# Remainder products behind the rounded ones in the first column tile of a dense stage, in a one-core decoder step

## The chip, the core and the metric

The kernel runs on one NeuronCore of a Trainium2 chip. The metric is device time in microseconds (us) of one execution. The profile shows the engines of the core: PE (TensorE, matrix products; PEld its weight loads), DVE (VectorE), ACT (ScalarE), POOL (GpSimd) and SP (the queue that issues most transfers), and the DMA engines.

## What is computed

One inference step of a decoder layer for two groups that share weights: 1024 prompt rows of width 1024, and 8 sample rows, each with 8192 cached positions. In the reference, cut to the parts around the change:

```python
xp = xp + merge_heads(fox_prompt(q, k, v, logf), sgu_prompt(u, z, w_s[l], b_s[l]), ...)
xp = xp + cross_attend(rmsnorm(xp, g_cross[l]), mk, mv, w_cq[l], w_co[l])   # q = xn @ w_cq
f, conv_p = conv_ffn(rmsnorm(xp, g_ffn[l]), ..., w_up[l], conv_w[l], conv_b[l], w_down[l])  # h = xn @ w_up
xp = xp + f
```

The same is done for the sample rows, whose attention reads the paged cache (`cache_k`, `cache_v`).

## The kernel before

The prompt rows are handled in two halves of 512. After the attention of both halves, each half goes through `merge`, `out_proj` (weights `w_o`), `cross` (cross-attention) and `ffn` (gated MLP with a convolution). All is written out by hand as Python generators; `yield` hands back a rough cost, and a loop at the end slips steps of the sample rows' work (`decode`: gather of cached keys, the product with the query at L1422 and the sum at L1426 on DVE, and later the product with the values at L1474 on PE) between steps of the prompt's. The recording layer then plans the whole program with a simulated timeline and fixes the order of the instructions on each engine; at run time every engine works through its own list in that order, and waits on semaphores.

Dense products are made nearly as exact as float32 by splitting each operand into a rounded part (float32r, written by ACT) and a remainder (written by DVE), and summing three products: rounded by rounded, and each remainder by the other's rounded part. For weights, `split` does this at L235 (ACT) and L236 (DVE), for scaled operands at L238 (ACT) and L239 (DVE). `gemm3` issues the three products, slice by slice, at L272 (rounded weights, rounded rows), L273 (rounded weights, remainder of the rows) and L274 (remainder of the weights, rounded rows).

`norm_T` prepares the normalised rows for `cross` and `ffn`. For the first 256 rows, then the other 256, it turns the rows with PE transposes (L1105), two of the eight 128-wide slices into one PSUM bank, and splits them from PSUM into `hs` (rounded) and `ls` (remainders). After each 256 rows it calls `first`, which issues the first column tile's 8 x 3 products for these rows, each with 256 columns; the later column tiles take all 512 rows at once. `first` runs in four places: `cross` and `ffn` of either half. In the second part of `ffn`'s rows, `ys[2:]` are scaled just before, by ACT (L1035 and L1036).

PSUM tiles come from the pools `ba` and `bb`; `u` are the SBUF buffers of the split rows, `wh` and `wl` those of the split weights, `kv` the buffers of the cached keys and values. L1006 adds a product to the rows (residual).

Of the kernel before, what the change touches and what calls it, by code (L numbers as in the profile page):

```python
# [45 lines left out]
G_MIX, G_CROSS, G_FFN, G_MEM, G_MERGE, B_S, CW, CB = 0, 8, 16, 24, 32, 40, 48, 48 + 132  # L46
# [32 lines left out]
def build(nc, tc, ctx, a, phases=None):  # L79
# [66 lines left out]
    def BK():  # L146
        turn_[0] += 1
        return BB() if turn_[0] % BR == BR - 1 else BA()

    MM = TR = BK  # L150
# [14 lines left out]
    mmul = nc.tensor.matmul  # L165
# [102 lines left out]
    def gemm3(out, pairs):  # L268

        n = len(pairs)  # L270
        for i, (sh, sl, mh, ml) in enumerate(pairs):
            mmul(out, sh, mh, start=(i == 0), stop=False)  # L272
            mmul(out, sh, ml, start=False, stop=False)  # L273
            mmul(out, sl, mh, start=False, stop=(i == n - 1))  # L274

    paused = [False]

# [841 lines left out]
    def cross(xt, sq):  # L1119
        mkn, mkT, mv, pp, pT = ([None] * MH for _ in range(5))  # L1120

        def fetch(h):
            hc = slice(h * MD, (h + 1) * MD)
            mkn[h] = T2().rearrange("p (a b) -> p a b", b=256)
            nc.sync.dma_start(mkn[h], mk_d[:, hc].rearrange("(a p) b -> p a b", p=P))
            mv[h] = T2().rearrange("p (a b) -> p a b", b=256)
            nc.sync.dma_start(mv[h], mv_d[:, hc].rearrange("(a p) b -> p a b", p=P))

        fetch(0)
        fetch(1)  # L1130

        ws = [wload(wpair(a["w_cq"], kk, 0, 512), 1024) for kk in range(4)]
        q2, ps0 = [], MM()

        def products(out, ws, dt_, hs, ls, c):
            cb = slice(dt_ * P, (dt_ + 1) * P)
            gemm3(
                out,
                [(ws[k // 2][0][:, k % 2, cb], ws[k // 2][1][:, k % 2, cb], hs[k][:, c], ls[k][:, c]) for k in range(8)],
            )  # L1140

        hs, ls = yield from norm_T(xt, G_CROSS, lambda hs, ls, c: products(ps0[:, c], ws, 0, hs, ls, c))
        r = rows_rstd(sq, 0, 4)
        rq = sm([P, 4], "rq", 2)
        nc.vector.tensor_scalar(rq, r, 1.0 / 16, None, op0=ALU.mult)
        oh, ol = [], []

        def keys(h):
            tr = TR()
            for dd in range(2):  # L1150
                for mt in range(2):
                    nc.tensor.transpose(
                        tr[:, dd * 256 + mt * P : dd * 256 + (mt + 1) * P], mkn[h][:, mt, dd * P : (dd + 1) * P], ident
                    )
            mkT[h] = T2().rearrange("p (a b) -> p a b", b=256)
            nc.scalar.activation(mkT[h], tr.rearrange("p (a b) -> p a b", b=256), AF.Copy)

        def weigh(h):
            mx = sm([P, 4], "cmx", 2)
            bs = sm([P, 4], "cbs", 2)  # L1160
            pp[h] = U([P, 4, 256])
            l4 = sm([P, 4], "cl", 2)
            r4 = sm([P, 4], "cr", 2)
            for g in range(2):
                sv = BK().rearrange("p (i m) -> p i m", m=256)
                for i2 in range(2):
                    i = g * 2 + i2
                    for dd in range(2):
                        mmul(sv[:, i2, :], q2[h][:, dd, i * P : (i + 1) * P], mkT[h][:, dd, :], start=(dd == 0), stop=(dd == 1))
                g2 = slice(g * 2, g * 2 + 2)  # L1170
                nc.vector.tensor_reduce(mx[:, g2], sv, axis=AX.X, op=ALU.max, negate=True)
                for i2 in range(2):
                    i = g * 2 + i2
                    nc.scalar.activation(bs[:, i : i + 1], mx[:, i : i + 1], AF.Copy, scale=rq[:, i : i + 1])
                for i2 in range(2):
                    i = g * 2 + i2
                    nc.scalar.activation(
                        pp[h][:, i, :], sv[:, i2, :], AF.Exp, bias=bs[:, i : i + 1], scale=rq[:, i : i + 1], accum_out=l4[:, i : i + 1]
                    )
            nc.vector.reciprocal(r4, l4)  # L1180
            for i in range(4):
                nc.scalar.activation(pp[h][:, i, :], pp[h][:, i, :], AF.Copy, scale=r4[:, i : i + 1])

        def turned(h):
            pT[h] = U([P, 2, 512])
            for mt in range(2):
                tr = TR()
                for i in range(4):
                    nc.tensor.transpose(tr[:, i * P : (i + 1) * P], pp[h][:, i, mt * P : (mt + 1) * P], ident)
                nc.scalar.activation(pT[h][:, mt, :], tr, AF.Copy)  # L1190

        def gather(h):
            oh2, ol2 = U([P, 2, 512], F32R), U([P, 2, 512], F32R)
            for dd in range(2):
                ps = BK()
                for mt in range(2):
                    mmul(ps, mv[h][:, mt, dd * P : (dd + 1) * P], pT[h][:, mt, :], start=(mt == 0), stop=(mt == 1))
                split(ps, oh2[:, dd, :], ol2[:, dd, :])
                oh.append(oh2[:, dd, :])
                ol.append(ol2[:, dd, :])  # L1200

        for n in range(2):
            if n:
                ws = [wload(wpair(a["w_cq"], kk, n * 512, 512), 1024) for kk in range(4)]
            for dt_ in range(4):
                if dt_ % 2 == 0:
                    q2.append(U([P, 2, 512]))
                if n or dt_:  # L1210
                    ps = MM()
                    products(ps, ws, dt_, hs, ls, slice(0, 512))
                else:
                    ps = ps0
                nc.scalar.activation(q2[-1][:, dt_ % 2, :], ps[:, :512], AF.Copy)
                yield 5.2
                if n and dt_ == 0:
                    keys(0)
                    keys(1)
                    fetch(2)  # L1220
                if n and 1 <= dt_ < 3:
                    weigh(dt_ - 1)
        keys(2)
        fetch(3)
        turned(0)
        yield 1
        weigh(2)
        yield 3
        gather(0)
        yield 4  # L1230
        keys(3)
        turned(1)
        yield 1
        weigh(3)
        yield 3
        gather(1)
        yield 4
        for h in (2, 3):
            turned(h)
            yield 1  # L1240
            gather(h)
            yield 4
        ys = []
        sq = yield from out_proj(a["w_co"], oh, ol, xt, ys=ys)
        return ys
# [2 lines left out]
    hlast = [const.tile([P, 2 * NF, 2], F32, tag=f"hlast{h}", name=f"hlast{h}") for h in range(2)]  # L1248

    def ffn(hf, xt, ys, late=None):  # L1250
        w0, pv0 = wload(a["w_up"][0], 1024), BK()

        def up(out, w, hs, ls, c):
            hv, lv = (w[q].rearrange("p (k c) -> p k c", c=P) for q in range(2))
            gemm3(out, [(hv[:, k, :], lv[:, k, :], hs[k][:, c], ls[k][:, c]) for k in range(8)])

        hs, ls = yield from norm_T(ys, G_FFN, lambda hs, ls, c: up(pv0[:, c], w0, hs, ls, c))
        if hf:

            fix = sm([P, 2 * NF, 2], "fix", 1)  # L1260
# [8 lines left out]
        for gi, gn in enumerate(GROUPS):  # L1269
            gh, gl = [], []  # L1270
            for f in range(f0, f0 + gn):
                hc2 = []
                for part in range(2):
                    ft = f + part * NF
                    cw = [gp[:, CW + i * 44 + ft : CW + i * 44 + ft + 1] for i in range(3)]
                    cb = gp[:, CB + ft : CB + ft + 1]
                    if ft:
                        w_, pv = wload(a["w_up"][ft], 1024), BK()
                        up(pv, w_, hs, ls, slice(0, 512))
                    else:  # L1280
                        pv = pv0
                    hc = T2()
                    nc.scalar.activation(hc, pv, AF.Identity, bias=cb, scale=cw[2])
                    nc.scalar.activation(hlast[hf][:, ft, :], pv[:, 510:512], AF.Copy)
                    nc.vector.scalar_tensor_tensor(hc[:, 1:], pv[:, :511], cw[1], hc[:, 1:], op0=ALU.mult, op1=ALU.add)
                    nc.vector.scalar_tensor_tensor(hc[:, 2:], pv[:, :510], cw[0], hc[:, 2:], op0=ALU.mult, op1=ALU.add)
                    if hf:
                        nc.vector.tensor_tensor(hc[:, 0:2], hc[:, 0:2], fix[:, ft, :], op=ALU.add)
                    hc2.append(hc)
                    yield 5.2  # L1290
# [11 lines left out]
            for n in range(2):  # L1302
                ws = []
# [8 lines left out]
                for i in range(4):  # L1312
                    tb = slice(i * P, (i + 1) * P)
                    ps = MM()
# [584 lines left out]
    for t in prompt():  # L1899
# [10 lines left out]
        while bgs and not held[0] and most and acc[0] >= PACE[phase[1] or phase[0]]:  # L1910
            most -= 1
            acc[0] -= PACE[phase[1] or phase[0]]
            w = next(bgs[0], None)
# [97 lines left out]
```

## Time and profile before

| | |
|---|---|
| Time, median of 3 runs | 1814.82 us (1810.97 to 1816.68) |
| Profiled execution | 1810.32 us, span of the core 1808.3 us |
| Granted PE clock, mean over the span | 0.989 |
| PE busy | 1741.4 us (96%), 9637 matmuls |
| DVE busy | 1396.9 us (77%) |
| ACT busy | 734.3 us (41%) |
| POOL busy | 501.8 us (28%) |
| Memory | 287 GB/s over the span |

The span is the time from the first to the last instruction of the core. Busy times overlap. In a group of instructions the fields are: line, engine, operation, output<-inputs, form, count; busy us and mean ns of one; idle time of the engine before them, and what ended it. In a timeline row: start in us, length in us, engine, line, operation, and in square brackets the idle time before it and its releaser. `PE bb L273` is the instruction of line 273 that writes a `bb` tile.

### The profile page before, as it was taken

The numbers are of one execution on the slowest core, as the hardware profiler recorded it, in microseconds if no ns is written. First come the engines' busy times: TensorE is split into PE (matmuls) and PEld (weight loads), VectorE is DVE, ScalarE is ACT, GpSimd is POOL, SyncE is SP. The second block draws the span as 40 slices with busy tenths as digits, with TensorE's granted clock in tenths as the row PEclk, the third lists the DMA queues.
The fourth block names the chain that finished last, engine by engine and source line by source line (L and its number), as shares of the span: only waits on it lengthen the run. The fifth ranks groups of instructions, "written<-read, shape, count | busy, mean of one in ns | idle before, by whom it ended". The sixth has DMA issues, their size and how long they took to land.

```text
span 1808.3 us, 25094 instructions
## 1 busy us (share of the span) xinstructions
PE 1741.4 (96%) x9637; PEld 1292.1 (71%) x9637; DVE 1396.9 (77%) x1729; ACT 734.3 (41%) x1378; POOL 501.8 (28%) x461
## 2 busy tenths in 40 slices
PE   8999999878999999999999999989999999999997
PEld 5887776656676767777777776766676678767875
DVE  4689658987788887999989899888875549855344
ACT  6332265465633544433323244235453333232332
POOL 1232333432133433223332233433322111001110
PEclk9999999998999999999999999999999999999999
DMA  7886888786597986778878788979878677568982
GB/s 290 304 304 230 293 316 331 261 278 196 213 404 268 346 315 252 264 280 338 321 278 317 267 313 329 383 285 349 325 283 314 246 289 253 183 260 295 358 314 81
DMA packets 157075, 521.06 MB, mean 288 GB/s; under 512 B 20875, under 2 KB 40843, under 8 KB 124187
## 3 DMA queue, kind: packets, MB, share of 16 engines
q0 software_dynamic: 57168, 341.14, 49.6%
q1 hardware_dynamic: 92874, 165.73, 26.2%
q10 hardware_dynamic: 6912, 12.59, 1.9%
q8 instruction: 76, 1.25, 0.3%
q14 instruction: 45, 0.36, 0.1%
HBM read 495.47 MB, written 23.93 MB: 287 GB/s over the span
## 4 chain that ended last, share of the span: by engine, by line
PE 53%; issue 8%; DMA 6%; DVE 5%; POOL 2%; ACT 2%; POOLq 0%; DVEq 0%; SPq 0%; ACTq 0%
PE ba L274 7%; PE ba L272 7%; PE ba L273 7%; PE bb L273 4%; PE bb L274 4%; PE bb L272 4%; PE dv L1474 4%; DMA kv<-cache_k,io 3%; DMA kv<-cache_v,io 2%; PE dv L321 1%; PE dv L1750 1%; PE ba L1055 1%; PE ba L1054 1%; PE ba L1056 1%; DVE s L1426 1%
## 5 line engine op out<-in xcount | busy, mean ns | idle before, releaser
L235 ACT ACTIVATE wh<-wr 128x1024 fp32r<-128x1024 f32 (+2 forms) x220 | 228.6, 1044 | 490.4 <-PE ba L273 157.7
L236 DVE TENSOR_TENSOR wl<-wr,wh 128x1024 fp32r<-128x1024 f32 (+2 forms) x220 | 262.3, 1198 | 174.0 <-PE ba L274 59.3
L1406 POOL DMA_INDIRECT kv<-cache_k,io x128 | 195.0, 1523 | 562.5 <-DVE s L1426 321.1
L1422 DVE TENSOR_TENSOR kv<-kv,d 128x1024 f32<-128x1024 f32 (+1 forms) x156 | 258.0, 1680 | 29.9 <-DMA kv<-cache_k,io 29.9
L1426 DVE TENSOR_REDUCE s<-kv 128x16 f32<-128x1024 f32 (+1 forms) x156 | 258.1, 1672 | 0.1
L1468 POOL DMA_INDIRECT kv<-cache_v,io x128 | 167.4, 1308 | 276.5 <-PE dv L1474 191.0
L273 PE MATMUL ba<-u,wh 128*128 128x512 f32 (+1 forms) x560 | 219.6, 392 | 1.8 <-DVE u L239 1.5
L272 PE MATMUL ba<-u,wh 128*128 128x512 f32 (+1 forms) x560 | 219.2, 393 | 1.7 <-ACT u L238 1.7
L274 PE MATMUL ba<-u,wl 128*128 128x512 f32 (+1 forms) x560 | 218.7, 392 | 0.0
L272 PE MATMUL ba<-wh,u 128*128 128x512 f32 (+1 forms) x495 | 186.9, 379 | 1.7 <-ACT u L235 1.7
L273 PE MATMUL ba<-wl,u 128*128 128x512 f32 (+1 forms) x495 | 185.5, 375 | 1.2 <-DVE wl L236 1.2
L274 PE MATMUL ba<-wh,u 128*128 128x512 f32 (+1 forms) x495 | 183.8, 376 | 0.0
L1474 PE MATMUL dv<-kv,s 128*32 128x512 f32 x1024 | 125.0, 598 | 2.9 <-DMA kv<-cache_v,io 2.9
L273 PEld LDWEIGHTS ba<-u,wh 128*128 128x128 f32 x560 | 106.0, 189 | 30.3 <-issue 5.2
L273 PE MATMUL bb<-u,wh 128*128 128x512 f32 (+1 forms) x304 | 118.6, 390 | 8.7 <-DVE u L239 8.7
L274 PEld LDWEIGHTS ba<-u,wl 128*128 128x128 f32 x560 | 105.9, 189 | 29.1 <-issue 6.1
L272 PEld LDWEIGHTS ba<-u,wh 128*128 128x128 f32 x560 | 105.9, 189 | 28.7 <-issue 4.0
L272 PE MATMUL bb<-u,wh 128*128 128x512 f32 (+1 forms) x304 | 118.5, 390 | 0.1
L274 PE MATMUL bb<-u,wl 128*128 128x512 f32 (+1 forms) x304 | 117.6, 387 | 0.0
L272 PEld LDWEIGHTS ba<-wh,u 128*128 128x128 f32 x495 | 93.0, 188 | 26.8 <-issue 6.9
L274 PEld LDWEIGHTS ba<-wh,u 128*128 128x128 f32 x495 | 92.8, 188 | 21.5 <-issue 3.8
L273 PEld LDWEIGHTS ba<-wl,u 128*128 128x128 f32 x495 | 93.1, 188 | 20.1 <-DVE wl L236 1.9
(432 smaller groups left out, 3251.0 us busy)
## 6 DMA issues: line engine op xcount, KB each, us to landing
wr<-w_up SPq DMA_DIRECT2D x88, 512.0 KB
kv<-w_up POOLq DMA_DIRECT2D x22, 1024.0 KB
wr<-w_down SPq DMA_DIRECT2D x40, 512.0 KB
kv<-w_down POOLq DMA_DIRECT2D x11, 1024.0 KB
wr<-w_in SPq DMA_DIRECT2D x16, 512.0 KB
wr<-w_o SPq DMA_DIRECT2D x16, 512.0 KB
wr<-w_cq SPq DMA_DIRECT2D x16, 512.0 KB
wr<-w_co SPq DMA_DIRECT2D x16, 512.0 KB
```

The lines of the kernel that those rows point to most:

```text
L235: nc.scalar.activation(h, src, AF.Copy)
L236: nc.vector.tensor_tensor(l, src, h.bitcast(F32), op=ALU.subtract)
L272: mmul(out, sh, mh, start=(i == 0), stop=False)
L273: mmul(out, sh, ml, start=False, stop=False)
L274: mmul(out, sl, mh, start=False, stop=(i == n - 1))
L321: mmul(ps[32 * j : 32 * j + 32, :w], xT[:, k, :] if nk == 8 else xT[:, k * 8 : k * 8 + 32], raw[:, q, j * w : (j + 1) * w], start=(k == 0) ...
L1054: mmul(pss[i], mh[k][:, tb], wh, start=(k == korder[0]), stop=False)
L1406: nc.gpsimd.indirect_dma_start(kv, None, a["cache_k"], off(kidx[:, b, ch : ch + 1]))
L1422: nc.vector.tensor_tensor(kvv[:, i : i + m, :], kvv[:, i : i + m, :], qb.unsqueeze(1).broadcast_to((P, m, 512)), op=ALU.mult)
L1426: nc.vector.tensor_reduce(s[:, ch * 4 + i : ch * 4 + i + m, :].rearrange("p k h -> p (k h)"), kvv[:, i : i + m, :].rearrange("p k (h d) -> ...
L1468: nc.gpsimd.indirect_dma_start(kv, None, a["cache_v"], off(kidx[:, b, ch : ch + 1]))
L1474: mmul(dv[32 * j : 32 * j + 32, :], s[:, ch * 4 : ch * 4 + 4, :].rearrange("p k h -> p (k h)"), kvv[:, j, :], start=(ch == 1), stop=(ch == ...
```

## The change

A second form of the three products, `gemm3_late`, takes a list of outputs. It issues, for every output, the products with rounded rows (with the rounded weights and with the weights' remainders) for all slices, and after those, for every output again, the products with the rows' remainders. The first column tile of `cross` and of `ffn` uses it, in both halves; every other tile keeps `gemm3`. The lists `begun` hold one tile each, so that the number of tiles that are begun in `norm_T` stays one. The sum of the same 24 products is accumulated in another order.

```diff
+    def gemm3_late(outs):
+
+        for out, pairs in outs:
+            for i, (sh, sl, mh, ml) in enumerate(pairs):
+                mmul(out, sh, mh, start=(i == 0), stop=False)
+                mmul(out, sl, mh, start=False, stop=False)
+        for out, pairs in outs:
+            for i, (sh, sl, mh, ml) in enumerate(pairs):
+                mmul(out, sh, ml, start=False, stop=(i == len(pairs) - 1))
...
-        q2, ps0 = [], MM()
-
-        def products(out, ws, dt_, hs, ls, c):
+        q2, begun = [], [MM() for _ in range(1)]
+
+        def pairs(ws, dt_, hs, ls, c):
             cb = slice(dt_ * P, (dt_ + 1) * P)
-            gemm3(out, [... for k in range(8)])
-
-        hs, ls = yield from norm_T(xt, G_CROSS, lambda hs, ls, c: products(ps0[:, c], ws, 0, hs, ls, c))
+            return [... for k in range(8)]
+
+        def first(hs, ls, c):
+            gemm3_late([(ps[:, c], pairs(ws, d, hs, ls, c)) for d, ps in enumerate(begun)])
+
+        hs, ls = yield from norm_T(xt, G_CROSS, first)
...
-        w0, pv0 = wload(a["w_up"][0], 1024), BK()
-
-        def up(out, w, hs, ls, c):
+        begun = {ft: (wload(a["w_up"][ft], 1024), BK()) for ft in (0,)}
+
+        def pairs(w, hs, ls, c):
             hv, lv = (w[q].rearrange("p (k c) -> p k c", c=P) for q in range(2))
-            gemm3(out, [(hv[:, k, :], lv[:, k, :], hs[k][:, c], ls[k][:, c]) for k in range(8)])
-
-        hs, ls = yield from norm_T(ys, G_FFN, lambda hs, ls, c: up(pv0[:, c], w0, hs, ls, c))
+            return [(hv[:, k, :], lv[:, k, :], hs[k][:, c], ls[k][:, c]) for k in range(8)]
+
+        def first(hs, ls, c):
+            gemm3_late([(pv[:, c], pairs(w, hs, ls, c)) for w, pv in begun.values()])
+
+        hs, ls = yield from norm_T(ys, G_FFN, first)
```

In the changed kernel the three lines of `gemm3_late` are 280 (rounded by rounded), 281 (remainder of the weights) and 284 (remainder of the rows).

More of the change, by code (lines that the diff above doesn't have):

```diff
@@ L1132, in cross @@
         ws = [wload(wpair(a["w_cq"], kk, 0, 512), 1024) for kk in range(4)]
-        q2, ps0 = [], MM()
-        def products(out, ws, dt_, hs, ls, c):
+        q2, begun = [], [MM() for _ in range(1)]
+        def pairs(ws, dt_, hs, ls, c):
             cb = slice(dt_ * P, (dt_ + 1) * P)
[L1137 to L1140, printed above, removed]
-        hs, ls = yield from norm_T(xt, G_CROSS, lambda hs, ls, c: products(ps0[:, c], ws, 0, hs, ls, c))
+            return [(ws[k // 2][0][:, k % 2, cb], ws[k // 2][1][:, k % 2, cb], hs[k][:, c], ls[k][:, c]) for k in range(8)]
+        def first(hs, ls, c):
+            gemm3_late([(ps[:, c], pairs(ws, d, hs, ls, c)) for d, ps in enumerate(begun)])
+        hs, ls = yield from norm_T(xt, G_CROSS, first)
         r = rows_rstd(sq, 0, 4)
@@ L1209, in cross @@
                     q2.append(U([P, 2, 512]))
-                if n or dt_:
+                if n or dt_ >= len(begun):
                     ps = MM()
-                    products(ps, ws, dt_, hs, ls, slice(0, 512))
+                    gemm3(ps, pairs(ws, dt_, hs, ls, slice(0, 512)))
                 else:
-                    ps = ps0
+                    ps = begun[dt_]
                 nc.scalar.activation(q2[-1][:, dt_ % 2, :], ps[:, :512], AF.Copy)
@@ L1276, in ffn @@
                     cb = gp[:, CB + ft : CB + ft + 1]
-                    if ft:
+                    if ft in begun:
+                        pv = begun.pop(ft)[1]
+                    else:
                         w_, pv = wload(a["w_up"][ft], 1024), BK()
-                        up(pv, w_, hs, ls, slice(0, 512))
-                    else:
-                        pv = pv0
+                        gemm3(pv, pairs(w_, hs, ls, slice(0, 512)))
                     hc = T2()
```

## The prediction

> **What bounds the kernel now.** I read the page first: busy time, then the chain that ended last.
>
> ```profile
> span 1808.3 us, 25094 instructions
> ...
> PE 1741.4 (96%) x9637; PEld 1292.1 (71%) x9637; DVE 1396.9 (77%) x1729; ACT 734.3 (41%) x1378; POOL 501.8 (28%) x461
> ...
> PE 53%; issue 8%; DMA 6%; DVE 5%; POOL 2%; ACT 2%; POOLq 0%; DVEq 0%; SPq 0%; ACTq 0%
> ```
>
> PE is occupied 96% of the span and carries the largest part of the chain; the last three matmul lines of the dense stages (L272 to L274) are the work that everything else serves. So a microsecond in which PE stands still is, at first sight, a microsecond of the kernel, and only PE's waits can be won. As many weight loads as matmuls were run (9637 each): every product loads its own weights, whatever stood before it, so regrouping products neither saves nor adds a load.
>
> The change touches four places, the first column tile after each of the four row normalisations. Next I read the groups of PE instructions in four stretches of 20 us that begin with the transposes L1105: cross-attention of the first half (546 to 566 us), its feed-forward (702 to 722), cross-attention of the second half (1177.5 to 1197.5) and its feed-forward (1340 to 1360). Of the first three answers stand the rows on which I build, in this order (one, two and one); in the fourth no wait for a remainder stands. The last field is PE's idle time before the group and what ended it.
>
> ```profile
> L273 PE MATMUL bb<-u,wh 128*128 128x256 f32 (+1 forms) x18 | 6.2, 345 | 2.7 <-DVE u L239 2.7
> L273 PE MATMUL ba<-u,wh 128*128 128x256 f32 (+1 forms) x18 | 6.6, 366 | 1.6 <-DVE u L239 1.5
> L1105 PE MATMUL ba<-cp,u 128*128 128x128 f32 x20 | 3.5, 288 | 1.1 <-ACT u L1035 1.1
> L273 PE MATMUL bb<-u,wh 128*128 128x256 f32 x10 | 4.2, 417 | 6.0 <-DVE u L239 6.0
> ```
>
> L273 is the product with the rows' remainder, and L239 on DVE makes that remainder. The waits that the change aims at are therefore 2.7, 1.5 and 6.0 us, 10.2 together. The 1.1 for the scaled rows (L1035) is not its subject. 10.2 us is the ceiling of the direct gain, 0.6% of the kernel. 0.3%, 5.4 us, is about what a measurement of this kernel can tell from no change.
>
> **The change, part by part.** It removes and adds no instruction: 16 products with rounded rows and 8 with remainders in each half of each tile, as before. It moves the eight remainder products behind the sixteen others, so that PE no longer stops at slice 1 while later rounded slices lie ready. What that is worth depends on what comes last in each place.
>
> *Second-half cross-attention* (the 6.0). The timeline, PE, then ACT, then DVE:
>
> ```profile
> 1183.22 0.39 PE L272 MATMUL bb<-u,wh 128*128 128x256 f32 x1
> 1189.11 0.58 PE L273 MATMUL bb<-u,wh 128*128 128x256 f32 x1 [5.50 <-DVE u L239]
> 1189.49 0.42 PE L274 MATMUL bb<-u,wl 128*128 128x256 f32 x1
> 1189.71 0.41 PE L272 MATMUL bb<-u,wh 128*128 128x256 f32 x1
> ...
> 1190.56 1.05 PE L1105 MATMUL ba<-cp,u 128*128 128x128 f32 x4
> 1191.27 0.56 PE L273 MATMUL bb<-u,wh 128*128 128x256 f32 x1
> ...
> 1194.56 0.28 PE L272 MATMUL bb<-u,wh 128*128 128x256 f32 x1
> 1194.68 0.28 PE L273 MATMUL bb<-u,wh 128*128 128x256 f32 x1
> ...
> 1194.91 0.60 PE L1105 MATMUL bb<-cp,u 128*128 128x128 f32 x4
> ...
> 1184.91 0.86 ACT L238 ACTIVATE u<-ba,gp 128x256 fp32r<-128x256 f32 x2
> 1186.32 2.35 DVE L1422 TENSOR_TENSOR kv<-kv,d 128x1024 f32<-128x1024 f32 x2
> 1189.83 0.86 DVE L239 SCALAR_TENSOR_TENSOR u<-ba,gp,u 128x256 fp32r<-128x256 f32 x2
> 1190.62 2.33 DVE L1426 TENSOR_REDUCE s<-kv 128x16 f32<-128x1024 f32 x2
> ...
> 1197.08 0.48 DVE L239 SCALAR_TENSOR_TENSOR u<-bb,gp,u 128x256 fp32r<-128x256 f32 x1 [0.54 <-ACT u L238]
> ```
>
> PE had run slice 0 and the first product of slice 1 when it stopped; 13 products with rounded rows were left, and ACT had rounded all eight slices by 1184.91 + 0.86 = 1185.8. A product takes 0.12 us (1194.56 to 1194.68), so these 13 take 1.6 us and fit into the 5.5 us of idle time. At 1189.1, when DVE delivers slice 1's remainder behind a decode product of 2.35 us, seven remainder products and three groups of four transposes are left. At the slow spacing of this place (0.22 from 1189.49 to 1189.71, 0.71 for a group of transposes from 1190.56 to 1191.27) that is 1.5 + 2.1 = 3.6 us; at the fast product spacing, 0.8 + 2.1 = 2.9. DVE's further remainders (the pair at 1189.83 ends at 1190.7) don't hold it up. The half tile then ends at 1192.0 to 1192.7 in place of 1194.9: 2.2 to 2.9 us. But the other half's remainders stand behind the decode sums on DVE (to 1192.9): six more at 0.39 (a pair takes 0.86, one 0.47) end at 1195.3, where now the last ends at 1197.6. So DVE passes on 2.3 at most. I take 2.0; bounds 1.0 (the transposes, now queued on PE behind the sixteen products, come no earlier) and 2.9.
>
> *First-half cross-attention* (the 2.7).
>
> ```profile
> 558.67 0.39 PE L273 MATMUL bb<-u,wh 128*128 128x256 f32 x1 [2.04 <-DVE u L239]
> 562.50 0.58 PE L273 MATMUL bb<-u,wh 128*128 128x256 f32 x1 [0.37 <-DVE u L239]
> ...
> 564.50 0.39 PE L272 MATMUL bb<-u,wh 128*128 128x512 f32 x1
> 561.97 0.47 DVE L239 SCALAR_TENSOR_TENSOR u<-bb,gp,u 128x256 fp32r<-128x256 f32 x1
> ```
>
> Here DVE sets the end: its last remainder is done at 562.44, and PE starts on it at 562.50. Behind it 14 products run until 564.50, nine of them with rounded rows. Those nine move ahead into the idle time: 9 x 0.12 = 1.1 us. The 2.04 itself isn't won, since the last remainder comes no sooner. Bounds 0 (their rounding is late too) and 2.7.
>
> *The two feed-forwards.* In the first, without the 1.5 us wait PE reaches the next transposes earlier and waits there for L1035, which ACT ends when it does now: 0, bounds -0.3 and 0.5. In the second nothing waits for a remainder: 0, bounds 0 and 0.5.
>
> Sum: 2.0 + 1.1 + 0 + 0 = 3.1 us.
>
> *The clock.* PE's granted clock falls to half after a stretch of 3.41 us in which PE did too little. A row of the stretches gives its bounds, its length, the busy time of PE, PEld, DVE, ACT and POOL, PE's clock, and the DMA's share and rate:
>
> ```profile
> 556.17:559.58 3.41, 1.37 (x8) 0.97 (x7) 3.41 (x7) 1.42 (x3) 1.00 (x1) 1.00 1.01 404
> 559.58:563.00 3.42, 3.05 (x10) 2.24 (x9) 3.42 (x6) 0.00 (x0) 0.00 (x0) 0.50 1.04 402
> 702.94:706.36 3.42, 1.93 (x14) 1.39 (x12) 3.42 (x7) 3.42 (x9) 1.62 (x2) 1.00 1.03 412
> 706.36:709.77 3.41, 1.52 (x9) 1.03 (x8) 1.59 (x4) 3.41 (x10) 0.54 (x1) 1.00 0.99 417
> 1184.20:1187.60 3.40, 0.00 (x0) 0.00 (x0) 3.40 (x6) 1.54 (x4) 0.92 (x1) 1.00 1.02 424
> 1187.60:1191.00 3.40, 1.89 (x9) 1.89 (x10) 3.40 (x8) 0.00 (x0) 1.94 (x1) 0.51 0.30 70
> 1191.00:1194.40 3.40, 3.40 (x17) 3.40 (x17) 2.86 (x5) 1.36 (x3) 0.95 (x1) 0.50 0.64 263
> ```
>
> After 1.93 us of work (702.94) the next stretch had the full clock, after 1.37 (556.17) and after none (1184.20) half: the threshold lies between 1.37 and 1.93. With most of the 13 products (1.6 us in all) the stretch of 1184.20 comes to that edge; with some of the nine (1.1 us) that of 556.17 may pass it. A stretch at half clock spaces products 0.22 instead of 0.12, and so loses about 3.41 x (1 - 0.12/0.22) = 1.5 us, unless a wait covers it, as DVE's last remainder at 562.44 does. I count a quarter of one such stretch, 0.4, bounds 0 and 2 x 1.5 = 3.0. [...]
>
> In all -3.5 us: 1810.32 for the profiled execution becomes 1806.8. That execution lies 4.5 us below the median of the runs (1814.82); from the median, 1811.3.
>
> **The rivals.**
>
> *The clock recovers as well (faster).* The stretches of 1187.60 and 1191.00 run at half clock now. If the early products before them suffice for the full clock, 2 x 1.5 = 3.0 us come on top of 3.5: -6.5, 1808.3, and up to -11 if the upper bounds of both attention terms hold too (0.9 and 1.6 more, and 2 of further waits and a third stretch). For it: 1.6 us more work in a stretch that had none. Against it: the threshold may be above that, and DVE is busy all of 1184 to 1191, so that PE may merely wait at full clock.
>
> *Given back (no change).* DVE, not PE, sets the pace where the change works (3.4 of 3.4 us busy in most of the stretches above). If the other half's remainders, or the next decode step's keys from memory, come when they come now, PE stops a little later: 0 to -1, about 1814.5. The same time follows if the scheduler had not kept the written order; in the built order it did, sixteen products first, with transposes between.
>
> *Reordered decode work (slower).* The scheduler planned the whole program anew. In the built order 322 of DVE's some 1730 instructions change place, though none by more than eleven. In the second half's output projection a decode product pair now goes ahead of a weight remainder (L236) and of a residual add (L1006).
>
> ```profile
> 1174.96 1.23 DVE L236 TENSOR_TENSOR wl<-wr,wh 128x1024 fp32r<-128x1024 f32 x1 [1.56 <-PE ba L1073]
> ```
>
> Each such swap delays what PE waits for by 2.3 us (L1422 above), if DVE has no slack; here it had 1.56 us. Two swaps without slack eat the gain, and from four on (4 x 2.35 - 3.5 = +5.9) the kernel is slower: 1820.7. For it: DVE is 77% busy. Against it: slack as in this row, and equal numbers of moves the other way.
>
> **How the numbers follow.** Forecast 40%, given back 10%, clock 32%, reordered 18%. Forecast and given back lie within 0.3%: 0.50; faster 0.32; slower 0.18. The likeliest case gives 1811.3. The range takes the clock rival down to -11 (1804) and the reordered one up to 1820, which leaves out about 1 in 10 on either side; the forecast alone, its bounds added up without the clock's (0.7 to 6.6 us), spans 1808.2 to 1814.1.
>
> **What would show it.** In the profile after: no wait of 5.5 us before slice 1's remainder product in the second-half cross-attention, but one of some 3 us further on, before line 284, and the tile done 2 to 3 us earlier; in the first half the wait for DVE moves behind the rounded products; in the first feed-forward the wait for L1035's rows grows by what the remainder wait loses. PE's busy time stays at 1741 us, less what the half clock gives back. Wrong would be: the same idle total in the four stretches, PE idle at new places between them, or more stretches at half clock.

## The result, and the profile after

| | before | after |
|---|---|---|
| median | 1815.41 us (1809.38 to 1821.46, 22 runs) | 1807.42 us (1802.23 to 1815.63, 22 runs) |
| ratio | | 0.9966, 95% interval 0.9955 to 0.9976 |
| profiled execution | 1810.32 us, clock 0.989 | 1812.65 us, clock 0.987 |

The changed kernel is faster by about 6 us (0.34% of 1815.4). A second measurement (e7 below) gave 0.9971. The ratio and its interval are formed from all runs of both kernels; they are not the quotient of the two medians, which lie 8.0 us apart. The two profiled executions rank the kernels the wrong way round: that of before lies 5 us under its median, that of after 5 us over. In the 253 runs of the experiments a run's time follows, within a kernel, its mean granted clock by about 1.1 us for each 0.001, and the 22 runs of the changed kernel above cover 0.984 to 0.994. So lengths from the traces are compared below stretch by stretch, and the gain is taken from the runs.

The page of after:

```profile
span 1810.9 us, 25097 instructions
...
PE 1741.1 (96%) x9637; PEld 1295.4 (72%) x9637; DVE 1398.3 (77%) x1729; ACT 735.3 (41%) x1378; POOL 503.7 (28%) x461
...
PE 50%; issue 8%; DMA 8%; DVE 7%; POOL 2%; ACT 1%; POOLq 0%; DVEq 0%; ACTq 0%
```

The matmuls and the instructions of DVE, ACT and POOL are as many as before (the three more in the total are none of these), and PE is busy as long as before. What moved is the order. The timeline of PE in the second cross half, with DVE's decode product of that moment as the last row:

```profile
1184.24 0.38 PE L280 MATMUL bb<-u,wh 128*128 128x256 f32 x1 [0.97 <-ACT u L238]
...
1186.01 0.39 PE L280 MATMUL bb<-u,wh 128*128 128x256 f32 x1 [0.56 <-ACT u L238]
...
1186.81 0.28 PE L284 MATMUL bb<-u,wh 128*128 128x256 f32 x1
1190.08 0.79 PE L284 MATMUL bb<-u,wh 128*128 128x256 f32 x2 [2.99 <-DVE u L239]
...
1193.94 0.56 PE L284 MATMUL bb<-u,wh 128*128 128x256 f32 x1
...
1187.28 2.35 DVE L1435 TENSOR_TENSOR kv<-kv,d 128x1024 f32<-128x1024 f32 x2
```

The wait of 5.50 us is now 2.99, and stands before line 284; 0.97 and 0.56 us of waits for ACT's rounding are new. All sixteen rounded products and slice 0's remainder are done by 1187.1. The last product of the half tile starts 15.25 us after the place's first transpose (1178.69), where it was 17.07 before (1194.79 - 1177.72), and twelve transposes for the next rows now stand ahead of it in place of eight.

The first cross half and the first feed-forward:

```profile
559.39 0.50 PE L273 MATMUL ba<-u,wh 128*128 128x512 f32 x1 [2.44 <-DVE u L239]
710.30 0.33 PE L1115 MATMUL ba<-cp,u 128*128 128x128 f32 x1 [3.09 <-ACT u L1045]
711.27 0.58 PE L280 MATMUL ba<-u,wh 128*128 128x256 f32 x1 [0.64 <-ACT u L238]
```

In the first, the wait is 2.44 us instead of 2.04 and 0.37, and now stands at a 512-column product that the planner put among these. In the second, the wait of 1.47 us for a remainder is gone, and the wait for the scaled rows has grown from 1.12 to 3.09.

The first transposes of the four places cut the span into stretches that can be compared. Before, then after:

```profile
546.12 1.03 PE L1105 MATMUL ba<-cp,u 128*128 128x128 f32 x8
702.22 0.60 PE L1105 MATMUL bb<-cp,u 128*128 128x128 f32 x4
1177.72 0.49 PE L1105 MATMUL ba<-cp,u 128*128 128x128 f32 x3
1340.90 0.60 PE L1105 MATMUL ba<-cp,u 128*128 128x128 f32 x4
```

```profile
546.82 1.03 PE L1115 MATMUL ba<-cp,u 128*128 128x128 f32 x8
704.94 0.60 PE L1115 MATMUL bb<-cp,u 128*128 128x128 f32 x4
1178.69 0.49 PE L1115 MATMUL ba<-cp,u 128*128 128x128 f32 x3
1339.84 0.60 PE L1115 MATMUL ba<-cp,u 128*128 128x128 f32 x4
```

From the first to the second place (cross of the first half) it is 156.1 before and 158.1 after, 2 us more. From the third to the fourth (cross of the second half) it is 163.2 and 161.2, 2 us less. Up to the first place every engine runs the same list, and behind it the planner has ordered the other work anew. So there are two candidates for the gain: the order of the products, and the order of all the rest.

### The profile page after: what moved, and what is told of

Its sections match the earlier page's. It is cut to its first block, busy times and chain, and to the rows that moved or that the text cites. A ratio compares the mean times of both kernels' runs of the same rounds, so it can differ in the third digit from the quotient of the medians.

```text
span 1810.9 us, 25097 instructions
## 1 busy us (share of the span) xinstructions
PE 1741.1 (96%) x9637; PEld 1295.4 (72%) x9637; DVE 1398.3 (77%) x1729; ACT 735.3 (41%) x1378; POOL 503.7 (28%) x461
## 4 chain that ended last, share of the span: by engine, by line
PE 50%; issue 8%; DMA 8%; DVE 7%; POOL 2%; ACT 1%; POOLq 0%; DVEq 0%; ACTq 0%
PE ba L272 6%; PE ba L274 6%; PE ba L273 6%; DMA kv<-cache_v,io 6%; PE dv L1487 3%; PE bb L272 3%; PE bb L273 3%; PE bb L274 3%; DVE s L1439 1%; DVE kv L1435 1%; DVE wl L236 1%; PE dv L331 1%; DMA kv<-cache_k,io 1%; PE dv L1763 1%; POOL kv L1419 1%
## 5 line engine op out<-in xcount | busy, mean ns | idle before, releaser
L1435 DVE TENSOR_TENSOR kv<-kv,d 128x1024 f32<-128x1024 f32 (+1 forms) x156 | 258.1, 1682 | 32.6 <-DMA kv<-cache_k,io 27.3
L273 PE MATMUL ba<-u,wh 128*128 128x512 f32 x528 | 208.5, 395 | 2.4 <-DVE u L239 2.4
L272 PE MATMUL ba<-u,wh 128*128 128x512 f32 x528 | 209.5, 397 | 0.0
L274 PE MATMUL ba<-u,wl 128*128 128x512 f32 x528 | 209.1, 396 | 0.0
L274 PEld LDWEIGHTS ba<-u,wl 128*128 128x128 f32 x528 | 99.2, 188 | 29.1 <-issue 5.7
L273 PEld LDWEIGHTS ba<-u,wh 128*128 128x128 f32 x528 | 99.3, 188 | 27.0 <-DVE u L239 2.6
L272 PEld LDWEIGHTS ba<-u,wh 128*128 128x128 f32 x528 | 99.5, 189 | 25.7 <-issue 4.0
L272 PE MATMUL bb<-u,wh 128*128 128x512 f32 x272 | 108.5, 399 | 0.0
L273 PE MATMUL bb<-u,wh 128*128 128x512 f32 x272 | 108.0, 397 | 0.0
L274 PE MATMUL bb<-u,wl 128*128 128x512 f32 x272 | 107.9, 397 | 0.0
```

Of the source, the lines that this page charges most:

```text
L1435: nc.vector.tensor_tensor(kvv[:, i : i + m, :], kvv[:, i : i + m, :], qb.unsqueeze(1).broadcast_to((P, m, 512)), op=ALU.mult)
```

## The experiments

Times are medians beside runs of the kernel before on the same chip; ratios are to those runs.

**e1 and e2: the new order in one stage only.** In the stage named the list is handed to `gemm3_late`, in the other to `gemm3`:

```diff
-            gemm3_late([(pv[:, c], pairs(w, hs, ls, c)) for w, pv in begun.values()])
+            for w, pv in begun.values():
+                gemm3(pv[:, c], pairs(w, hs, ls, c))
```

> Only the cross stage's first tile takes the new order; the ffn's first tile has the order of before again. Theory (the rounded products fill the waits for the remainders in the two cross places, the ffn places give about nothing): ratio to before 0.9966 to 0.998, that is the whole gain of the full change; in the trace the second cross half shows the wait before L284 of about 3 us and the tile's last product 1 to 2.5 us after the last remainder. Rival, the new plan of the work around (not the order of the products) gives the gain: a ratio that lies anywhere between 0.995 and 1.003, with the waits at the first tiles as in the full change. Rival, the ffn places carry half of the gain: 0.9983.

> Only the ffn's first tile takes the new order; the cross stage's first tile has the order of before again. Theory: no gain, ratio 0.9995 to 1.0005, the 5.5-us wait in the second cross half is there again. Rival, the ffn places carry half: 0.9983. Rival, the new plan: anywhere between 0.995 and 1.003.

e1: 1813.82, ratio 1.0009 (0.9998 to 1.0021). e2: 1817.09, ratio 1.0021 (1.0007 to 1.0035). In e1 the wait of the second cross half has shrunk as in the full change:

```profile
1187.82 0.80 PE L284 MATMUL bb<-u,wh 128*128 128x256 f32 x2 [2.62 <-DVE u L239]
```

And yet nothing is won; e2, where nothing was to be won, loses 3.8 us. The theory missed both. Both lie in what the rival of a new plan allowed (0.995 to 1.003), which is too wide to be a test.

**e3: the remainder last within each slice.** In `gemm3_late` the second loop is dropped, and the remainder product follows the two others of its slice:

```diff
                 mmul(out, sl, mh, start=False, stop=False)
-        for out, pairs in outs:
-            for i, (sh, sl, mh, ml) in enumerate(pairs):
                 mmul(out, sh, ml, start=False, stop=(i == len(pairs) - 1))
```

> Both first tiles, but the product with the remainder is only put last within each slice (three products a slice, slice after slice), so that at most two more rounded products stand before the first wait for a remainder. Theory: the waits for the remainders stay, 5.2 to 5.5 us in the second cross half and 2 us in the first; ratio 0.9995 to 1.0003. Rival, any new order of these products makes the program around it be planned anew and that gives the gain: 0.996 to 0.998 as in the full change.

1807.91, ratio 0.9979 (0.9965 to 0.9992), not what the theory expected, with the big wait in place:

```profile
1184.41 0.58 PE L282 MATMUL bb<-u,wh 128*128 128x256 f32 x1 [5.33 <-DVE u L239]
```

So a kernel can win 3.8 us without filling the wait, and another can fill it and win none. Each of these small edits makes the planner order the program anew, and the results scatter by 4 us either way.

**e4: two tiles begun.** `range(2)` in place of `range(1)` for `begun` in `cross`, and `(0, NF)` in place of `(0,)` in `ffn`.

> The new order, with two tiles begun instead of one in both stages: the rounded products of two tiles (32 per half tile instead of 16) stand before the first product with a remainder. Theory: in the second cross half the rounded products of the second tile lie in the 3.0-us wait that the full change leaves, 16 of 0.12 us = 1.9 us, and in the first half the 2.4-us wait shrinks by as much; together 2 to 4 us below the full change, ratio to before 0.9945 to 0.9960. Rival, what bounds the place is not the remainders but the clock that is halved there: then PE does the same work at half speed and the ratio is that of the full change, 0.9966. Rival, the second tile's weights or bank come late or keep a bank from the work around: above 0.998.

1814.03, ratio 1.0012 (0.9993 to 1.0031): the theory missed it. PE's idle time in the 20 us from each place is the least of all (0.8, 3.7, 3.2 and 0.6 us, against 2.4, 3.7, 4.5 and 2.5 in e7, the changed kernel again), and the kernel is no faster than before. Its trace has a new wait that begins 72 us behind the third place. PE's row, then ACT's:

```profile
1258.01 6.59 PE L1179 MATMUL ba<-t,u 128*128 128x256 f32 x16 [7.79 <-ACT t L1166]
...
1255.93 1.06 ACT L235 ACTIVATE wh<-wr 128x1024 fp32r<-128x1024 f32 x1 [3.11 <-DMA wr<-w_co]
...
1257.37 0.59 ACT L1166 ACTIVATE t<-ba 128x512 f32<-128x512 f32 x1
```

PE waits for a copy by ACT, and in ACT's list a rounding of weights stands ahead of it that itself waits 3.11 us for the weights. So here too the order of the rest weighs against what the places win. e4 also runs 96 more matmuls (9733), as a tile that is begun takes 256 columns at a time. What each of the two costs was not measured.

**The order of the rest held still.** To part the two candidates, the program is planned once in each order of the products, the two plans are taken as lists of instructions for every engine, and the kernel proper is chained to a list put together from them:

```diff
+    for e, q in plan.items():
+        for x, y in zip(q, q[1:]):
+            tc.add_manual_dep(traced[y], x, info, reason="plan")   # y behind x on engine e
```

In the stretch of a first tile PE's list takes the tile's products from one plan; everything else on PE, and all of ACT, DVE, POOL and SP, comes from the other. In the first two kernels the row transposes among the products counted as part of the rest.

> The new order of the products in all four places, but every other instruction of every engine keeps the order that it has in the kernel before (the order is written out and each engine's list is chained to it). Theory of the prediction (the rounded products lie in the waits for the remainders): the whole gain of the order is here, 2.5 to 3.5 us, ratio 0.9981 to 0.9986; the second cross half shows a wait of about 3 us before L284 in place of 5.5 us before L273. Rival, the gain of the full change comes from the decode and prompt work that the planner orders anew behind the first place: ratio 0.9997 to 1.0005 here.

> The reverse: the three products of each slice stand together as in the kernel before, but every other instruction of every engine has the order of the changed kernel. Theory of the prediction: no gain, ratio 0.9995 to 1.0005, and the wait of 5 us or more before the remainder's product is there again. Rival, the new order of the other work gives the gain: 0.9966 to 0.9982, the same as the full change.

> The changed kernel itself, measured beside the two. It was 0.9966 (0.9955 to 0.9976) of the kernel before, with a mean clock of 0.9888; at the same granted clock the two differ by 3.2 us, 0.9982. Theory and rival both expect 0.9965 to 0.9985; it says whether the two kernels beside it, with one half of the change each, add up to it.

e5: 1812.47, ratio 0.9992 (0.9978 to 1.0006). e6: 1819.74, ratio 1.0031 (1.0014 to 1.0049). e7: 1810.18, ratio 0.9971 (0.9957 to 0.9985). Neither half alone is the change: e5 lies between its theory and its rival, and e6 misses both, being slower than before. In e5 the wait stayed:

```profile
1184.67 1.09 PE L1124 MATMUL ba<-cp,u 128*128 128x128 f32 x4 [5.21 <-DVE rq L1165]
```

It is now a transpose that waits. Before, four transposes for the next 256 rows stood between slice 3's products; they wait for DVE, and in e5 they were left there, with nine of the sixteen rounded products behind them. The planner of the full change had put them behind the rounded products. So e5 left undone a part of what the change does.

**e8 to e10: the transposes as well.** In e8 and e9 the transposes among the products go with them.

> As e5 (new order of the products, the rest in the order of before), but the row transposes that stand among a first tile's products also take the place that they have in the changed kernel: in the second cross half they stand behind the rounded products. e5 had kept them in front of the last rounded products, and there the 5.2-us wait stayed. Theory: the gain is in the tile's own stretch, products and transposes together: the 5.2-us wait shrinks to about 3 us and the ratio falls from 0.9992 to 0.9975 to 0.9983. Rival, the order of the other work behind the first places gives the rest: ratio 0.9988 to 0.9996, as e5.

> As e6 (products slice by slice, the rest in the order of the changed kernel), with the row transposes too in the place that they have in the kernel before. Theory: without the new order there is no gain, 0.9995 to 1.0005. Rival, the order of the other work has a gain of its own: 0.9975 to 0.9985. Third, that order fits only the new order of the products, as e6 with 1.0031 looks: 1.0015 to 1.0035 again.

> The remainder's product last within each slice, as in e3, but every other instruction keeps the order of the kernel before. e3, planned anew, had 0.9979 with the waits for the remainders all but unchanged. If that gain came from the order of the other work, this kernel has none: 0.9995 to 1.0005. If it came from the products themselves: 0.9975 to 0.9985.

e8: 1811.61, ratio 0.9984 (0.9969 to 1.0000). e9: 1814.87, ratio 1.0015 (0.9999 to 1.0030). e10: 1814.53, ratio 1.0003 (0.9987 to 1.0019). The waits of the second cross half in e8 and e10:

```profile
1184.83 0.61 PE L282 MATMUL bb<-u,wh 128*128 128x256 f32 x2 [2.97 <-DVE u L239]
```

```profile
1187.62 0.80 PE L282 MATMUL bb<-u,wh 128*128 128x256 f32 x2 [5.47 <-DVE u L239]
```

e10 answers e3: with the rest held still, the order within a slice shows no gain, so e3's 3.8 us needed the rest planned anew. e8 gives the worth of the new order with the rest of before, about 2.9 us (0 to 5.6); the interval covers its theory and its rival, and by time e8 cannot be told from e5, though the wait fell from 5.21 to 2.97 us. The rest of the changed kernel does not pay by itself (e9).

**e11 and e12: the new rest in the second half only.** On every engine the two plans hold the same instructions up to a point some 30 us ahead of the third place. The list is the plan of before up to there, that of the change behind it.

> The new order of the products, with the rest in the order of the kernel before up to some 30 us ahead of the second cross half, and from there in the order of the changed kernel (both lists hold the same instructions up to that point on each engine). In the traces the stretch from the first row transpose of the first cross half to that of the first ffn half takes 156.1 and 156.1 us with the order of before (the kernel before, e8) and 158.1 and 158.7 us with the new one (the changed kernel, e7), the stretch from the second cross half to the second ffn half 163.2 and 164.9 against 161.2 and 160.9 us. Theory: the order of the rest that comes with the change loses 2 us in the first stretch and wins 2 to 4 us in the second; with the better of each this kernel lies 1.5 to 3 us below the changed kernel, ratio 0.9950 to 0.9963. Rival: such differences of single executions are the clock's, and the order of the rest has no part: 0.9984 as e8.

> The same order of the rest as e11, but the three products of each slice stand together as in the kernel before, with the row transposes in their old place. Against e11 it is the price of the order of the products with all else the same; against the kernel before it is the price of the order of the rest in the second half. Theory: the order of the products carries 2 to 3.5 us, so 0.9975 to 0.9990 here. Rival, the order of the rest is worth something only with the new order of the products (e9 was at 1.0015): 0.9998 to 1.0010.

e11: 1806.69, ratio 0.9959 (0.9946 to 0.9972). e12: 1813.40, ratio 0.9996 (0.9983 to 1.0010). e11 is as its theory had it and excludes its rival; e12 lies nearer to its rival. All in one table, ratios to the kernel before:

| rest of the program | old order of the products | new order | worth of the new order |
|---|---|---|---|
| as before | 1 | 0.9984 (e8) | -0.16%, 2.9 us |
| new in the second half | 0.9996 (e12) | 0.9959 (e11) | -0.37%, 6.7 us |
| new | 1.0015 (e9) | 0.9971 (e7), 0.9966 | -0.44 to -0.49%, 8 to 9 us |

The new order pays in each row. By the means of the listed runs, with 1.96 standard errors, it is worth 2.5 ± 2.2, 6.9 ± 1.9 and 8.5 ± 2.9 us. The new rest in the second half adds 4.5 us to it (e8 to e11; 5.6 ± 2.6 by the means), but next to nothing without it (e12). That the order is worth more with the new rest is therefore likely: the second row lies 4.4 ± 2.9 us above the first. The new rest in the first half costs 1.3 to 2.2 us (e11 to the changed kernel), which is within the error of the runs (1.9 ± 2.2); the traces below show it more clearly. The intervals of e11 and the changed kernel overlap, so that e11 is the better one is likely and not shown.

**Where the rest acts.** In the second cross half the next marks are the decode products with the values and the cross-attention. PE's rows of before, of e8 and of after:

```profile
1255.51 1.92 PE L1474 MATMUL dv<-kv,s 128*32 128x512 f32 x16 [0.64 <-DMA kv<-cache_v,io]
1266.29 0.66 PE L1189 MATMUL ba<-cp,u 128*128 128x128 f32 x4 [0.90 <-ACT u L1177]
1283.39 1.12 PE L1197 MATMUL bb<-u,t 128*128 128x512 f32 x2 [0.58 <-ACT u L1190]
```

```profile
1173.43 0.49 PE L1124 MATMUL ba<-cp,u 128*128 128x128 f32 x3
...
1249.47 1.92 PE L1497 MATMUL dv<-kv,s 128*32 128x512 f32 x16 [1.24 <-DMA kv<-cache_v,io]
...
1262.04 0.66 PE L1209 MATMUL ba<-cp,u 128*128 128x128 f32 x4 [1.61 <-ACT u L1197]
...
1280.82 1.12 PE L1217 MATMUL bb<-u,t 128*128 128x512 f32 x2 [0.58 <-ACT u L1210]
```

```profile
1256.08 1.92 PE L1487 MATMUL dv<-kv,s 128*32 128x512 f32 x16 [1.56 <-DMA kv<-cache_v,io]
1266.32 0.66 PE L1199 MATMUL ba<-cp,u 128*128 128x128 f32 x4 [0.36 <-ACT u L1187]
...
1282.93 1.12 PE L1207 MATMUL bb<-u,t 128*128 128x512 f32 x2 [0.58 <-ACT u L1200]
```

Counted from each kernel's first transpose of the place, PE reaches the wait for the values (row start less the wait) at 77.15 us before, 74.80 in e8 and 75.83 after: the tile has won 2.35 and 1.3 us. The last row starts at 105.67, 107.39 and 104.24. Before and after need the same 28.5 us between the two marks; e8 needs 32.6. In this execution of e8 the gain is given back: to longer waits than before's for the values (1.24 us against 0.64; after has 1.56) and for ACT (1.61 us against 0.90 and 0.36), and to a stretch at half clock behind the latter. The windows of e8, with columns as in the prediction:

```profile
1260.20:1263.60 3.40, 1.12 (x6) 0.69 (x7) 3.40 (x4) 3.40 (x12) 1.46 (x1) 1.00 1.02 408
1263.60:1267.00 3.40, 3.40 (x9) 2.69 (x9) 3.40 (x6) 2.21 (x8) 1.35 (x1) 0.50 1.00 402
```

In the first cross half it is the new rest that waits. After, and e8 (which has the rest of before):

```profile
620.46 1.92 PE L1487 MATMUL dv<-kv,s 128*32 128x512 f32 x16 [1.91 <-DMA kv<-cache_v,io]
623.23 1.99 PE L1179 MATMUL bb<-t,u 128*128 128x256 f32 x8 [0.85 <-ACT t L1166]
632.47 0.66 PE L1199 MATMUL bb<-cp,u 128*128 128x128 f32 x4 [1.21 <-ACT u L1187]
633.81 3.72 PE L1179 MATMUL ba<-t,u 128*128 128x256 f32 x16 [0.68 <-ACT t L1166]
```

```profile
543.25 1.03 PE L1124 MATMUL ba<-cp,u 128*128 128x128 f32 x8
...
582.03 1.92 PE L1497 MATMUL dv<-kv,s 128*32 128x512 f32 x16 [1.41 <-DMA kv<-cache_v,io]
```

The row of before at the same wait:

```profile
585.22 1.92 PE L1474 MATMUL dv<-kv,s 128*32 128x512 f32 x16 [1.17 <-DMA kv<-cache_v,io]
```

With the new rest PE no longer waits at the first batch of decode products with the values (e8's row), but longer at a later one and at the cross-attention behind it: 4.65 us in after, while e8 has 1.41 us and some 1.2 us later on. The same two stretches, from the first transpose of each cross half to that of the ffn behind it, in all the traces in which the rest is one of the two orders (us):

| | products | rest, first half | first stretch | rest, second half | second stretch |
|---|---|---|---|---|---|
| before | old | before | 156.1 | before | 163.2 |
| e10 | last in slice | before | 156.6 | before | 165.0 |
| e5 | new, transposes kept | before | 156.0 | before | 165.5 |
| e8 | new | before | 156.1 | before | 164.9 |
| e11 | new | before | 155.4 | new | 160.8 |
| e12 | old | before | 156.1 | new | 162.6 |
| after | new | new | 158.1 | new | 161.2 |
| e7 | new | new | 158.7 | new | 160.9 |
| e6 | old, transposes kept | new | 160.6 | new | 162.8 |
| e9 | old | new | 160.6 | new | 161.1 |

Each row is one execution, but the two orders of the rest do not overlap in either stretch: the new one takes 158.1 to 160.6 against 155.4 to 156.6 us in the first, and 160.8 to 162.8 against 163.2 to 165.5 in the second. The order of the products shows less: with the rest of before the first stretch is the same within 1.3 us, and in the second e8 and e5 are 1.7 and 2.3 us longer than before, as e10 is by 1.8; with the new rest the new order is 1.9 to 2.5 us shorter in the first and up to 2.0 in the second.

## Why the prediction was right, and where it was not

The forecast was -3.5 us; measured were -6.2 (0.9966) and -5.3 (0.9971), just about the 0.3% that it set as the bound of a gain: the first lies in its case "faster", to which it gave 0.32, the second in that of the forecast. The move of the wait came as described, but by the ratios about half of the gain is the reordered rest, which it had only as a loss; that the sum still fell so near is in part luck. By its steps:

- *Second cross half, 2.0 us (1.0 to 2.9).* Right in place and size: the 5.5-us wait became one of 2.97 to 2.99 us before line 284, the half tile ends 1.8 us earlier (15.25 against 17.07), and the next mark on PE is reached 1.3 us earlier in the changed kernel and 2.35 in e8.
- *First cross half, 1.1 us.* About half: e8 reaches its wait for the values at 582.03 - 1.41 = 580.62, 37.4 us after its first transpose at 543.25; before, that took 37.9 us. That wait then takes nearly half of it: PE goes on 38.8 us after the transpose, before after 39.1.
- *First feed-forward, 0 (-0.3 to 0.5).* Right in the mechanism: the wait moved to the scaled rows. 1.47, 1.12 and 0.64 us became 3.09 and 0.64, 0.5 us more in all.
- *Second feed-forward, 0 (0 to 0.5 won).* Missed: 1.5 us of PE's waits became 2.0 in e8, 2.5 in e7 and e11 and 4.2 in after. In e11 all of it is for ACT's rounding (0.54, 1.62 and 0.33 us, against 0.20 and 0.90 before): the rounded products, now close behind one another, wait for ACT.
- *Clock, 0.4 (0 to 3.0).* Low, but inside its bounds, by the run lists: the new order with its transposes (e7, e8, e11) had a mean clock of 0.9885 over 34 runs, the kernel before 0.9875 over 113, and the old order with a new rest (e9, e12) 0.9863 over 24, each of the small groups known to 0.0009 (the first 22 runs of the changed kernel had 0.9888, e6 0.9835). At 1.1 us for each 0.001 that is some 1 us against before, hardly more than the error, and 2.4 us against e9 and e12. But it did not come where the rival looked for it. In the second cross half the stretch of 1182.10 holds 2.38 us of work (2.27 in that of 1180.80 before), and the next, the one in which the wait begins, holds 1.08 (none before) and was again followed by half clock (0.50):

```profile
1182.10:1185.50 3.40, 2.38 (x19) 1.97 (x17) 3.40 (x7) 3.16 (x8) 1.70 (x2) 1.00 0.91 340
1185.50:1188.90 3.40, 1.08 (x7) 0.88 (x7) 3.40 (x5) 1.24 (x4) 1.26 (x1) 1.00 0.97 400
1188.90:1192.30 3.40, 2.22 (x10) 2.22 (x11) 3.40 (x8) 0.47 (x1) 1.61 (x1) 0.50 0.32 87
```

- *The sum of these, -3.1 without the clock.* e8 measures -2.9 us (0 to 5.6). That the two agree is in part luck: e8's trace shows no gain by the marks (156.1 us as before in the first cross half, 1.7 more in the second), and its runs had a mean clock of 0.9886 against 0.9873 of the runs beside them, worth about 1.4 us at 1.1 for each 0.001.
- *Its signs of being wrong.* It named the same idle total in the four stretches, PE idle at new places, or more half clock. PE's idle time in the 20 us from each place adds up to 13.7 us before, 15.0 in after, 13.1 in e7, 13.2 in e11 and 12.7 in e8: the waits were moved more than removed. At half clock PE ran for 40.4 us of the profiled span before and for 48.5 in after, with mean clocks of 0.989 and 0.987; e7 had 0.987. So both profiles of the changed kernel show such signs while the runs show a gain; single executions decide little here, as the scatter in the last section shows.
- *The rest planned anew.* Here the account was incomplete. The prediction knew that the planner had reordered the program and counted that only as a rival that slows. The new rest works both ways: 1.3 to 2.2 us lost in the first half (e11 against the changed kernel), 4.5 us won in the second (e8 against e11), on balance 2.4 to 3.3 us won over e8 (3.7 ± 2.7 by the means). The mechanism that the rival named, decode work ahead of a weight remainder on DVE, was not what showed: the waits that grew are for the gathered values and for ACT.
- *Given back.* Partly true where the rest was kept: e8's trace loses in the cross-attention what its tile had won. With the new rest it passes through.

Not settled is why the new rest pays only with the new order, if it does. The traces show that in after the time from the wait for the values to the cross-attention stays at 28.5 us and in e8 grows; each is one execution, and a stretch at half clock more or less is up to 1.7 us of it (an estimate, half of 3.41). Nor do the stretches of the profiled executions add up to 6 us, for the reason given with the result.

## What to carry to other kernels

When a planner orders the program, no edit is local: plan it both ways, chain the kernel to one plan, and change only the lines in question, before a gain of some tenths of a per cent is put down to a mechanism. Move all that stands in the queue between the moved products (here transposes that wait for DVE) or the wait just changes its instruction (5.21 us before a transpose in e5, 2.97 with the transposes moved as well in e8). The idle time at the edited place is not the gain: the kernel with the least of it here (e4) was no faster than before.

## What the runs showed of the hardware

Half clock came here not only behind the 5.5-us wait. In e8's window from 1260.20 PE had work for 1.12 of 3.40 us, its longest pause was 1.61 us, and the next 3.40 us ran at half clock (0.50). In the changed kernel's window from 1185.50 PE had work for 1.08 us before a pause of 2.99 us began, and the next window ran at 0.50 too. In the prediction's row of 706.36 it was 1.52 us of work with no pause above 1.12. What these share with the rows of 556.17 and 1184.20 is little work in a window (1.37 us and none), wherever the pauses lie.

The profiled executions of before and after can be counted through. In each, every change of PE's clock between 10 and 1790 us lies on a grid of 3.413 us, and that part of the span was cut into windows along it. Of the windows at full clock, all 6 with at most 1.37 us of PE work were followed by half clock, 9 of the 16 with 1.48 to 1.99 us, and none of the 995 with 2.17 us or more. So these two executions show no single threshold "between 1.37 and 1.93", as the prediction had it, but an overlap: seven windows with 1.75 to 1.93 us of work were followed by full clock, and one with 1.99 us and no pause above 1.06 was followed by half clock (after, from 349.24). Of the 23 windows at half clock, the 8 followed by another had 1.94 to 2.98 us of work, and the 15 followed by full clock 2.92 to 3.41.

The same program up to the first place took 543.3 to 546.8 us in the profiled executions of before, after, e7, e8, e9, e11 and e12. That 3.6-us scatter, without any edit, is more than half of the whole effect. Of this time PE ran at half clock for 20.5 us in before (546.12) and 23.9 in after (546.82). The shortest of the seven (e8, 543.25) had the highest mean clock over its span, 0.991 against 0.987 to 0.989 in the others.
